# Output projection by seven products of quarters, added onto each other in PSUM

## The chip, the cores and the metric

The kernel runs on one core of one Trainium2 chip. The metric is the device time of one execution in microseconds (us); less is better. The number given for a kernel is the median over its runs.

## What is computed

One pre-norm layer of a decoder, 512 tokens of 1024 channels, all in float32, then a last norm:

```python
u = rmsnorm(x, ln1_g[i]);  proj = u @ w_in[i]          # q, k, v, pool, z, xbc, dt, gates
y_a = dilated_attention_mixer(q, k, v, rel_bias) @ w_a[i]
y_b = pool_mixer(pool_in, pool_w[i], pool_scale[i]) @ w_b[i]
y_c = ssd_mixer(...) @ w_c[i]
merged = gates[:, :, 0] * y_a + gates[:, :, 1] * y_b + gates[:, :, 2] * y_c
x = x + merged @ w_o[i]                                 # the output projection
x = x + conv_ffn(rmsnorm(x, ln2_g[i]), ...)
return rmsnorm(x, final_g)
```

The change concerns `merged @ w_o`, a product of 512x1024 by 1024x1024, and what lies next to it.

## The kernel before

**Products in three parts.** A float32 operand is split in a high half (rounded to float32r by a ScalarE cast, `cast`, L187) and a low half (operand minus high half, VectorE, `low`, L220, subtraction at L216). A product is high x high + high x low + low x high: `mm3` (L229) issues these as three sweeps over the 128-row blocks k, all added up in one PSUM bank.

**Jobs.** The work is a list of `Job`s in program order (`program`, L1442). A job has a weight piece of at most 1 MB (128 partitions x 2048) and a body. Before the body of job n, `prepare` (L1660) issues the low half of the weights of job n+1, the cast of those of n+2 (in two halves, put off to the next two calls of `step`), and the load of those of n+3. There are two buffers for raw weights, three for high halves, two for low halves. If a job is marked `late`, its body calls `prepare` itself. If it has a `then`, this runs right after its low half (L223), and a `form` gives the weights in place of a load (L190).

**Order.** The instructions of PE, ScalarE, VectorE and GpSimd go out in the order of the code; the DMA queue (SP) has an order of the scheduler. `step` (L157) runs one stretch of each generator in `running`: this is how small work is spread between blocks of matmuls.

**The stage before.** `branch_jobs(2, w_c, ..., last=True)` (L1152) has four jobs of two chunks m of 128 channels. A chunk is 24 matmuls; then VectorE multiplies by the gate (L1159), adds to the merged sum `MG[m]` (L1160), and, as this is the last branch, ScalarE and VectorE split `MG[m]` into high and low (L1163, L1164).

**The output projection** (`wo_jobs`, L1182) has eight jobs. Tokens are rows of the output, in four blocks tb of 128. For each pair of blocks and each half h of the 1024 output columns there are two jobs, one for each half of the contraction; `w_o` is thus loaded and split twice. After the second one VectorE adds the bank to the residual `X1[tb, h]` (L1185). After h = 0 follows `norm_early` (L456: ScalarE sums the squares, VectorE takes the mean, GpSimd multiplies by the gain), and after h = 1 `norm_late` (L465) and `norm_turn` (L446): scaling of both halves to `u`, eight transposes on TensorE, a ScalarE copy (L453) and a VectorE subtraction (L454). Their results are the operands of the FFN's up projection, whose first two jobs (`opening`, L1364) start with tokens 0 to 255 while the norm of the last two blocks is finished.

**Seven products.** Other parts of the kernel already form a product of 2x2 quarters by seven products (Winograd's form): `sums_of` (L319) makes the sums of the left side, `diff` (L337) differences of weight quarters, and the products' results are combined from SBUF copies (`sevens`, L341; `down_group`, L1281).

Buffers: 128x512 tiles in SBUF come from one pool of 54 (`T`, L108), PSUM banks for products from one of four (`MM`, L111), and two 1 MB buffers hold the second weight halves of a seven (`ypool`).

Of the kernel before, what the change touches and what calls it, by code (L numbers as in the profile page):

```python
# [83 lines left out]
def trunk(ctx: ExitStack, tc, out, x, rel_bias, ln1_g, w_in, b_gate, w_a, pool_w, pool_scale, w_b,  # L84
# [41 lines left out]
    waiting, running = [], []  # L126
# [99 lines left out]
    def wsrc(w, k0, k1, c0, c1):  # L226
        return w[k0 * P:k1 * P, c0:c1].rearrange("(k p) c -> p k c", p=P)

    def mm3(ps, wh, wl, xh, xl, ks, first=True, last=True, flip=False):  # L229

        n, total = 0, 3 * len(ks)
        for a, b in ((wh, xh), (wh, xl), (wl, xh)):
            for k in ks:
                l, r = (b(k), a(k)) if flip else (a(k), b(k))
                pe.matmul(ps, l, r, start=first and n == 0, stop=last and n == total - 1)  # L235
                n += 1

    def chunk_a(ps, ws, j, xh, xl, ks, lo=0, hi=S, k0=0):
# [98 lines left out]
    def diff(out, a, b):  # L337
        dve.tensor_tensor(out, a, b, OP.subtract)
        return out
# [113 lines left out]
            act.copy(hh, pv)  # L453
            dve.tensor_sub(ul[:, 4 * h:4 * h + 4, tb * P:(tb + 1) * P], pv, hh.bitcast(F32))  # L454

    def norm_early(t, g):  # L456
# [3 lines left out]
        dve.tensor_scalar(v0, ss, 1.0 / D, EPS, OP.mult, OP.add)  # L460
        pool.tensor_tensor(xg, t, g[:, :S], OP.mult)
        V0.append(v0)
        return v0, xg

    def norm_late(t, g, v0, outs, last=False):  # L465

        ss, v, sq, r, rt = (small(n, [P, 1]) for n in ("ss", "v", "sq", "r", "rt"))
        squares(act, t, ss)
        act.activation(sq, ss, AF.Sqrt, bias=v0, scale=1.0 / D)
        xg = T("xg")  # L470
        dve.tensor_tensor(xg, t, g[:, S:], OP.mult)
        dve.scalar_tensor_tensor(v, ss, 1.0 / D, v0, OP.mult, OP.add)
        yield xg
        dve.reciprocal(r, sq)
        dve.scalar_tensor_tensor(rt, r, v, r, OP.mult, OP.mult)
        dve.tensor_scalar(rt, rt, -0.5, 1.5, OP.mult, OP.add)
        if not last:
            for o, src in outs(xg):
                dve.tensor_scalar(o, src, r, rt, OP.mult, OP.mult)
# [411 lines left out]
    XS, YT, Y = {}, {}, {}  # L891
# [260 lines left out]
    def branch_jobs(b, w, parts, nk, last=False, more=()):  # L1152
        def evac(m, ps):
            if b == 1:
                MG[m] = T("yo")
                act.copy(MG[m], ps)
                return
            s = SG[b, m]
            dve.tensor_tensor(s, s, ps, OP.mult)  # L1159
            (dve if last else pool).tensor_tensor(MG[m], MG[m], s, OP.add)  # L1160
            if last:
                h, l = T("mgh", F32R), T("mgl", F32R)
                act.copy(h, MG[m])  # L1163
                dve.tensor_sub(l, MG[m], h.bitcast(F32))  # L1164
                MH[m] = (h, l)

        return jobs_a(w, 0, 8, lambda k: parts[k][0], lambda k: parts[k][1], nk, evac,
                      width=256 if nk > 4 else 512, more=more)


    X1 = {}
# [10 lines left out]
    def wo_jobs(pair, h):  # L1182
        def evac(tb, ps):
            t = X1[tb, h]
            dve.tensor_tensor(t, t, ps, OP.add)  # L1185
            if h == 0:
                nxt[tb] = norm_early(t, nxt["g2"])
                return
# [5 lines left out]
            it = norm_late(t, nxt["g2"], v0, lambda xg1: ((us[0], xg0), (us[1], xg1)))  # L1194
            next(it)

            def rest():
                next(it, None)
                yield
                norm_turn(us, nxt["uh"], nxt["ul"], tb)  # L1200

            if pair == 0:
                r = rest()
                next(r)
                running.append(after(1, r))
# [8 lines left out]
        return jobs_b(lambda k0, k1: [wsrc(w_o, k0, k1, h * S, h * S + S)], S,  # L1214
                      lambda k, tb: MH[k][0][:, tb * P:(tb + 1) * P],
                      lambda k, tb: MH[k][1][:, tb * P:(tb + 1) * P], KD, evac,
                      blocks=(2 * pair, 2 * pair + 1), turn_over=pair == 1 and h == 1)


    ACTS = {}  # L1220
# [193 lines left out]
    def early(tb):  # L1414
        yield
        fin[tb] = norm_early(X1[tb, 0], fin["g"])
# [25 lines left out]
    def program():  # L1442
        yield from jobs_a(w_in, C_POOL, 8, uhk, ulk, KD, pool_evac)
        yield Call(lambda: waiting.append(rows_of_bias()))
        yield from v_jobs(0)
        yield from qk_jobs(0)
        yield from pool_out_job()
        yield Call(lambda: attend(0))
        yield Call(lambda: waiting.insert(3, ssd_prep()))
        for i, job in enumerate(branch_jobs(1, w_b, YB, 8, more=range(7))):  # L1450
            if i == 3:
                yield Call(lambda: running.extend(after(p, sums_of_u(p)) for p in range(4)))
            yield job
# [24 lines left out]
        yield Call(finish)  # L1478
        yield from branch_jobs(2, w_c, YT, 8, last=True)
        yield Call(load_x1)  # L1480
        for pair in range(2):
            for h in range(2):
                yield from wo_jobs(pair, h)
            if pair == 0:
# [235 lines left out]
```

## Time and profile before

| what | value |
|---|---|
| median of 3 runs | 1033.97 us (1033.73 to 1034.62) |
| profiled execution, its own time | 1034.33 us |
| its span, first to last instruction | 1032.0 us |
| TensorE busy | 1021.4 us (99%) |
| VectorE busy | 714.3 us (69%) |
| ScalarE busy | 498.7 us (48%) |
| last branch's matmuls | from 583.30 us |
| output projection's matmuls | from 626.82 us |
| up projection's first matmul | 672.64 us |

A row of the timeline has start, duration, engine, line, operation, tile written <- tiles read, shapes and count; in brackets stands the idle time of the engine before it and what ended it. PE is TensorE, DVE VectorE, ACT ScalarE, POOL GpSimd, SP the queue that issues the loads. In the waits, a row has who waited for whom, the sum in us, how often, and the longest.

### The profile page before, as it was taken

Reading aid. Unit: us, or ns where it says so; the run is one execution under the profiler, and the core shown is the slowest. Engines: PE = TensorE matmul, PEld = TensorE weight load, DVE = VectorE, ACT = ScalarE, POOL = GpSimd, SP = SyncE. Lnnn points to the kernel's source line nnn. Section 1 sums busy time; section 2 is a strip of 40 time slices with the busy share of each in tenths; the row PEclk is TensorE's granted clock in tenths of the full one; section 3 lists DMA queues with packets and bytes.
Section 4 is the critical chain, followed back from the end, with each engine's and each line's share of the span. In section 5 each row is a group of like instructions: output and inputs, shape, how many; then the busy total and the mean of one; then the engine's idle time right before and its main releaser. Section 6 shows DMA issues by size and latency. Waiting matters only on the chain.

```text
span 1032.0 us, 13285 instructions
## 1 busy us (share of the span) xinstructions
PE 1021.4 (99%) x5276; PEld 858.8 (83%) x5276; DVE 714.3 (69%) x948; ACT 498.7 (48%) x800; POOL 133.5 (13%) x114
## 2 busy tenths in 40 slices
PE   9999999999999999999999999999999999999997
PEld 8998877899888887788888888898888888888885
DVE  6553566788756648666688856767778759876776
ACT  6432545454674363567575324545445544445334
POOL 1770000000000001100044501101111100111002
PEclk9999999999999999999999999999999999999999
DMA  8444312134322364551253625543231233412222
GB/s 256 148 128 139 107 57 75 31 88 137 123 82 82 94 155 110 132 144 45 79 157 121 202 82 205 175 143 114 82 123 41 85 119 98 148 41 82 82 82 82
DMA packets 112300, 115.52 MB, mean 112 GB/s; under 512 B 5203, under 2 KB 97174, under 8 KB 112239
## 3 DMA queue, kind: packets, MB, share of 16 engines
q1 hardware_dynamic: 111647, 113.83, 36.1%
q8 instruction: 41, 0.67, 0.3%
q10 hardware_dynamic: 592, 0.86, 0.2%
q14 instruction: 20, 0.16, 0.0%
HBM read 110.87 MB, written 2.22 MB: 110 GB/s over the span
## 4 chain that ended last, share of the span: by engine, by line
PE 90%; DVE 5%; ACT 3%; issue 1%; DMA 1%; ACTq 0%; DVEq 0%
PE pa L235 30%; PE pu L235 22%; PE pb L235 12%; PE pd L235 7%; PE pqk L235 6%; PE pa L1571 2%; PE pq L235 2%; PE pu L1375 1%; PE ps L740 1%; PE pt L769 1%; PE ppw L235 1%; PE po L781 1%; DVE wl L216 1%; DVE xs L1130 1%; PE py L1054 1%
## 5 line engine op out<-in xcount | busy, mean ns | idle before, releaser
L216 DVE TENSOR_TENSOR wl<-raw,wh 128x2048 fp32r<-128x2048 f32 (+3 forms) x93 | 213.5, 2297 | 47.8 <-ACT wh L196 42.7
L196 ACT CAST wh<-raw 128x1024 fp32r<-128x1024 f32 (+3 forms) x184 | 183.6, 1017 | 40.9 <-DMA raw<-in_ffn_w_down_dram 13.2
L1248 DVE SCALAR_TENSOR_TENSOR hc<-pu,fcol,hc 128x510 f32<-128x510 f32 x88 | 65.8, 748 | 48.4 <-ACT hc L1245 46.8
L235 PE MATMUL pa<-uh,wh 128*128 128x512 f32 x384 | 98.4, 398 | 0.0
L235 PE MATMUL pa<-ul,wh 128*128 128x512 f32 x384 | 94.9, 389 | 0.0
L235 PE MATMUL pa<-uh,wl 128*128 128x512 f32 x384 | 94.8, 389 | 0.0
L235 PEld LDWEIGHTS pa<-ul,wh 128*128 128x128 f32 x384 | 72.1, 188 | 15.1
L235 PEld LDWEIGHTS pa<-uh,wl 128*128 128x128 f32 x384 | 72.1, 188 | 15.0
L235 PE MATMUL pu<-uh,wh 128*128 128x512 f32 (+1 forms) x352 | 83.6, 379 | 0.0
L235 PE MATMUL pu<-uh,wl 128*128 128x512 f32 (+1 forms) x352 | 83.5, 379 | 0.0
L235 PE MATMUL pu<-ul,wh 128*128 128x512 f32 (+1 forms) x352 | 83.5, 379 | 0.0
L235 PEld LDWEIGHTS pa<-uh,wh 128*128 128x128 f32 x384 | 70.4, 188 | 14.8 <-issue 1.0
L235 PEld LDWEIGHTS pu<-ul,wh 128*128 128x128 f32 x352 | 64.2, 188 | 12.5
L235 PEld LDWEIGHTS pu<-uh,wl 128*128 128x128 f32 x352 | 64.2, 188 | 12.5
L235 PEld LDWEIGHTS pu<-uh,wh 128*128 128x128 f32 x352 | 64.1, 188 | 12.4
L1245 ACT ACTIVATE hc<-pu,fcol,fcol 128x512 f32<-128x512 f32 x40 | 31.2, 780 | 79.7 <-PE pu L235 79.7
L1253 POOL TENSOR_TENSOR hc<-hc 128x512 f32<-128x512 f32 x22 | 31.7, 1442 | 288.6 <-DVE hc L1248 253.6
L1022 POOL TENSOR_TENSOR xd<-xc,dtz 128x512 f32<-128x512 f32 x6 | 6.4, 1062 | 356.1 <-issue 307.7
L762 ACT ACTIVATE sb<-sb,nmls 128x128 f32<-128x128 f32 (+1 forms) x72 | 30.1, 419 | 30.4 <-DVE nmls L759 17.7
L1146 ACT ACTIVATE sg<-pa,col 128x512 f32<-128x512 f32 x24 | 16.5, 687 | 45.0 <-PE pa L235 44.9
L1250 ACT ACTIVATE hc<-hc 128x512 f32<-128x512 f32 x22 | 13.9, 632 | 41.0 <-DVE hc L1248 41.0
L216 DVE TENSOR_TENSOR wl<-w,wh 128x2048 fp32r<-128x2048 f32 (+1 forms) x14 | 29.9, 2135 | 5.3 <-ACT wh L196 5.3
(379 smaller groups left out, 1891.0 us busy)
## 6 DMA issues: line engine op xcount, KB each, us to landing
raw<-in_w_in_dram SPq DMA_DIRECT2D x25, 1024.0 KB, 5.4
raw<-in_ffn_w_up_dram SPq DMA_DIRECT2D x22, 1024.0 KB, 5.2
raw<-in_w_o_dram SPq DMA_DIRECT2D x8, 1024.0 KB, 6.5
raw<-in_w_in_dram SPq DMA_DIRECT2D x14, 512.0 KB, 3.9
raw<-in_ffn_w_down_dram SPq DMA_DIRECT2D x6, 1024.0 KB, 5.2
raw<-in_w_in_dram SPq DMA_DIRECT2D x6, 768.0 KB
raw<-in_w_b_dram SPq DMA_DIRECT2D x4, 1024.0 KB, 5.0
al<-ad SPq DMA_DIRECT2D x16, 256.0 KB, 7.1
```

Source lines behind the costliest of these rows:

```text
L196: act.copy(job.high[:, :, o], job.raw[:, :, o])
L216: (eng or dve).tensor_tensor(l[:, :, o], job.raw[:, :, o], h[:, :, o].bitcast(F32), OP.subtract)
L235: pe.matmul(ps, l, r, start=first and n == 0, stop=last and n == total - 1)
L740: pe.matmul(pss[i][:, o:o + w * P], q[r, n * P:(n + 1) * P], k[r, kb * P:(kb + w) * P], start=True, stop=True)
L762: act.activation(sb[:, off:off + w * P], sb[:, off:off + w * P], AF.Exp, bias=nm[:, n, h:h + 1], accum_out=ls[:, n, h:h + 1])
L769: pe.transpose(pt[:, o:o + P], sb[:, o:o + P], eye)
L1146: act.activation(s, ps, AF.Sigmoid, bias=col[:, o:o + 1])
L1245: act.activation(t, ps, AF.Identity, bias=ff["c1"][:, ff["b"] + m:ff["b"] + m + 1], scale=fw(2, m))
L1248: dve.scalar_tensor_tensor(t[:, sh:], ps[:, :S - sh], fw(k, m), t[:, sh:], OP.mult, OP.add)
L1250: act.activation(t, t, AF.Silu)
L1253: pool.tensor_tensor(a, a, t, OP.mult)
L1571: pe.matmul(first[2 * n + j][:, lo:hi], a[:, k, j * P:(j + 1) * P], b[:, k, lo:hi], start=a is wh and b is uh and k == 0, stop=a is wl and ...
```

## The change

The eight jobs of the output projection become seven. The contraction is in pairs of neighbouring 128-channel blocks (even block = first half, odd block = second half), the tokens in halves of 256 and the output columns in halves of 512. Each product is one job of two blocks of 128 tokens, 12 matmuls each. The products `two`, `five` and `three` use the two banks B, `one`, `six`, `seventh` and `four` the two banks A. `five` starts its banks afresh; `three`, `six`, `seventh` and `four` add onto what their banks hold (`onto=True`), and VectorE adds the bank's present value to the residual after every product. The weights come from four loads of 1 MB, and the differences are made in place by VectorE as `then` of four jobs. The left side's sums are made by `merged` in the steps after each pair of chunks of the last branch. The residual x is loaded one job earlier, and `ff_cols` is called before `three`. For blocks 0 and 1 the norm is finished after `six`; for 2 and 3, whose column half 1 is ready first, after `four`, with the halves' parts exchanged.

```diff
-    def mm3(ps, wh, wl, xh, xl, ks, first=True, last=True, flip=False):
+    def mm3(ps, wh, wl, xh, xl, ks, first=True, last=True, flip=False, onto=False):
+        first = first and not onto
...
             if last:
-                h, l = T("mgh", F32R), T("mgl", F32R)
-                act.copy(h, MG[m])
-                dve.tensor_sub(l, MG[m], h.bitcast(F32))
-                MH[m] = (h, l)
+                running.append(merged(m))
...
+    def merged(m):
+        a, p = MG[m], m // 2
+        if m % 2 == 0:
+            t = T("mg0", F32R)
+            act.copy(t[:, LO], a[:, LO])
+            dve.tensor_sub(t[:, HI], a[:, LO], t[:, LO].bitcast(F32))
+            MH[0, p] = (t[:, LO], t[:, HI])
+            return
+        h, l = T("mgh", F32R), T("mgl", F32R)
+        act.copy(h, a)
+        it = sums_of(MG[m - 1], a, T("msh", F32R), T("msl", F32R),
+                     lambda j, h, l: MH.__setitem__((j, p), (h, l)))
+        next(it)
+        dve.tensor_sub(l, a, h.bitcast(F32))
+        MH["A12", p] = (h[:, LO], l[:, LO])
+        MH["A22", p] = (h[:, HI], l[:, HI])
+        yield
+        yield from it
...
+        def job(j, raw, form, bank, use, more=False):
+            def body(ws):
+                wh, wl = ws
+                if not A:
+                    for b in (B, A):
+                        b.extend(MM("pb") for _ in range(2))
+                ps = {"A": A, "B": B}[bank]
+                if new.late:
+                    late_split.append(new.prepare(later=True))
+                parts = [MH[{"A11": 0}.get(j, j), p] for p in range(4)]
+                for i in range(2):
+                    o = slice(i * P, (i + 1) * P)
+                    mm3(ps[i], lambda k: wh[:, k, :], lambda k: wl[:, k, :],
+                        lambda k: parts[k][0][:, o], lambda k: parts[k][1][:, o], range(4),
+                        flip=True, onto=more)
+                    use(i, ps[i])
+                    step()
...
+        def p2(i, ps):
+            add(i, 0, ps)
+            early(i, 0)
+        def p6(i, ps):
+            add(i, 1, ps)
+            finished(i, 1)
+        def p7(i, ps):
+            add(2 + i, 1, ps)
+            early(2 + i, 1)
+        def p4(i, ps):
+            add(2 + i, 0, ps)
+            finished(2 + i, 0)
+        one = job("A11", quarter(0, 0), None, "A", lambda i, ps: add(i, 0, ps))
+        two = job("A12", quarter(1, 0), None, "B", p2)
+        five = job(1, None, lambda: one.raw, "B", lambda i, ps: add(2 + i, 1, ps))
+        three = job(4, None, lambda: W[1], "B", lambda i, ps: add(i, 1, ps), more=True)
+        six = job(2, None, lambda: one.raw, "A", p6, more=True)
+        seventh = job(3, None, lambda: W[0], "A", p7, more=True)
+        four = job("A22", None, lambda: two.raw, "A", p4, more=True)
+        one.then = lambda: diff(one.raw, W[0], one.raw)
+        five.then = lambda: diff(one.raw, W[1], one.raw)
+        three.then = lambda: diff(W[0], W[1], W[0])
+        six.then = lambda: diff(two.raw, two.raw, one.raw)
+        four.late = True
+        return load, [one, two, five, three, six, seventh, four]
...
-        yield from branch_jobs(2, w_c, YT, 8, last=True)
-        yield Call(load_x1)
-        for pair in range(2):
-            for h in range(2):
-                yield from wo_jobs(pair, h)
-            if pair == 0:
+        load, wo = wo_group()
+        yield Call(load)
+        for i, job in enumerate(branch_jobs(2, w_c, YT, 8, last=True)):
+            if i == 3:
+                yield Call(load_x1)
+            yield job
+        for i, job in enumerate(wo):
+            if i == 3:
                 yield Call(ff_cols)
+            yield job
```

In `finished`, the late norm of blocks 0 and 1 is now queued whole (`running.append(after(1, rest()))`), where before its scaling was issued at once.

More of the change, by code (lines that the diff above doesn't have):

```diff
@@ L234, in mm3 @@
                 l, r = (b(k), a(k)) if flip else (a(k), b(k))
-                pe.matmul(ps, l, r, start=first and n == 0, stop=last and n == total - 1)
+                pe.matmul(ps, l, r, start=first and n == 0, stop=last and n == total - 1,
+                          skip_group_check=onto)
                 n += 1
@@ L454, in norm_turn, with norm_early @@
             dve.tensor_sub(ul[:, 4 * h:4 * h + 4, tb * P:(tb + 1) * P], pv, hh.bitcast(F32))
-    def norm_early(t, g):
+    def norm_early(t, g, half=slice(0, S)):
         ss, v0, xg = small("ss", [P, 1]), cpool.tile([P, 1], F32, name=f"v0_{len(V0)}"), T("xg")
@@ L460, in norm_early, with norm_late @@
         dve.tensor_scalar(v0, ss, 1.0 / D, EPS, OP.mult, OP.add)
-        pool.tensor_tensor(xg, t, g[:, :S], OP.mult)
+        pool.tensor_tensor(xg, t, g[:, half], OP.mult)
         V0.append(v0)
         return v0, xg
-    def norm_late(t, g, v0, outs, last=False):
+    def norm_late(t, g, v0, outs, last=False, half=slice(S, D)):
         ss, v, sq, r, rt = (small(n, [P, 1]) for n in ("ss", "v", "sq", "r", "rt"))
@@ L470, in norm_late @@
         xg = T("xg")
-        dve.tensor_tensor(xg, t, g[:, S:], OP.mult)
+        dve.tensor_tensor(xg, t, g[:, half], OP.mult)
         dve.scalar_tensor_tensor(v, ss, 1.0 / D, v0, OP.mult, OP.add)
@@ L1180, in load_x1, with wo_group, load, add @@
                 sp.dma_start(t, x[tb * P:(tb + 1) * P, h * S:(h + 1) * S])
[L1182 to L1188, printed above, removed]
+    def wo_group():
+        quarter = lambda two, h: w_o[:, h * S:(h + 1) * S].rearrange(
+            "(k two p) c -> two p k c", two=2, p=P)[two]
+        W, A, B = [], [], []
+        def load():
+            for two in range(2):
+                W.append(ypool.tile([P, 4, S], F32, name="w3", tag="xs"))
+                sp.dma_start(W[two], quarter(two, 1))
+        def add(tb, h, ps):
+            dve.tensor_tensor(X1[tb, h], X1[tb, h], ps, OP.add)
+        def early(tb, h):
+            nxt[tb] = norm_early(X1[tb, h], nxt["g2"], slice(h * S, h * S + S))
+        def finished(tb, h):
             if "uh" not in nxt:
@@ L1193, in evac @@
             us = [T("u0"), T("u1")]
-            it = norm_late(t, nxt["g2"], v0, lambda xg1: ((us[0], xg0), (us[1], xg1)))
+            it = norm_late(X1[tb, h], nxt["g2"], v0, lambda xg: ((us[1 - h], xg0), (us[h], xg)),
+                           half=slice(h * S, h * S + S))
             next(it)
@@ L1200, in rest @@
                 norm_turn(us, nxt["uh"], nxt["ul"], tb)
-            if pair == 0:
-                r = rest()
-                next(r)
-                running.append(after(1, r))
+            if tb < 2:
+                running.append(after(1, rest()))
             elif tb == 2:
@@ L1212, in evac @@
                 late_split.pop(0)()
[L1214 to L1217, printed above, removed]
+        def job(j, raw, form, bank, use, more=False):
[15 more added lines that the diff above has]
+                    step()
+            new = Job([raw] if raw is not None else [], 4, S, body)
+            new.form = form
+            if raw is None:
+                new.load = lambda: None
+            return new
@@ L1478, in program @@
         yield Call(finish)
-        yield from branch_jobs(2, w_c, YT, 8, last=True)
-        yield Call(load_x1)
-        for pair in range(2):
-            for h in range(2):
-                yield from wo_jobs(pair, h)
-            if pair == 0:
+        load, wo = wo_group()
[6 more added lines that the diff above has]
+            if i == 3:
                 yield Call(ff_cols)
+            yield job
         loads, groups = zip(*(down_group(base) for base in range(0, KS, 8)))
```

## The prediction

> **What bounds the kernel now.** The page comes first, then the busy times by stretch for the last third's two stages.
>
> ```profile
> span 1032.0 us, 13285 instructions
> ...
> PE 1021.4 (99%) x5276; PEld 858.8 (83%) x5276; DVE 714.3 (69%) x948; ACT 498.7 (48%) x800; POOL 133.5 (13%) x114
> ...
> PEclk9999999999999999999999999999999999999999
> ...
> PE 90%; DVE 5%; ACT 3%; issue 1%; DMA 1%; ACTq 0%; DVEq 0%
> ```
>
> ```profile
> 583.30:626.82 43.52, 43.52 (x193) 36.05 (x192) 25.30 (x26) 11.01 (x14) 5.35 (x3) 1.00 0.35 115
> 626.82:672.64 45.82, 45.82 (x212) 37.94 (x210) 31.98 (x47) 24.11 (x38) 5.18 (x4) 1.00 0.59 202
> ```
>
> The columns of the second fence are the stretch, its length, and the busy time of PE, weight loads, DVE, ACT and POOL. TensorE is never idle in either, the third branch (583.30 on) or the output projection (626.82 on). So a matmul fewer is worth its full time, **as long as VectorE keeps up**. VectorE has 18.2 us free in the first stretch and 13.8 us in the second. The question is what the change does with those 32 us.
>
> The timeline of PE gives the price of the matmuls and where the stage ends:
>
> ```profile
> 626.82 1.07 PE L235 MATMUL pb<-wh,mgh 128*128 128x512 f32 x4
> 627.73 1.07 PE L235 MATMUL pb<-wh,mgl 128*128 128x512 f32 x4
> ...
> 654.03 1.91 PE L450 MATMUL uT<-eye,u 128*128 128x128 f32 x16
> ...
> 672.64 2.08 PE L1375 MATMUL pu<-uh,wh 128*128 128x256 f32 x16
> ...
> 676.47 1.04 PE L450 MATMUL uT<-eye,u 128*128 128x128 f32 x8
> 677.44 2.18 PE L1375 MATMUL pu<-uh,wl 128*128 128x256 f32 x16
> ```
>
> Four matmuls start every 0.907 us, so one costs 0.227 us and a block of 12 costs 2.72 us.
>
> **What goes.** Before: 8 jobs x 2 blocks x 12 = 192 matmuls. After: 7 x 2 x 12 = 168. 24 x 0.227 = **5.44 us** of TensorE time goes, with four 1 MB loads and one weight split.
>
> **What comes, by VectorE's queue.** The engines run in the order of the code, so I lay the new order end to end with durations of before.
>
> ```profile
> 610.71 0.69 DVE L1159 TENSOR_TENSOR sg<-sg,pa 128x512 f32<-128x512 f32 x1
> 611.50 0.69 DVE L1160 TENSOR_TENSOR yo<-yo,sg 128x512 f32<-128x512 f32 x1
> ...
> 616.14 0.69 DVE L1159 TENSOR_TENSOR sg<-sg,pa 128x512 f32<-128x512 f32 x1 [2.58 <-PE pa L235]
> ```
>
> ```profile
> 635.18 0.69 DVE L1185 TENSOR_TENSOR x<-x,pb 128x512 f32<-128x512 f32 x1 [0.37 <-PE pb L235]
> 636.66 0.15 DVE L460 TENSOR_SCALAR v<-ss 128x1 f32<-128x1 f32 x1 [0.79 <-ACT junk L437]
> ...
> 641.27 4.49 DVE L216 TENSOR_TENSOR wl<-raw,wh 128x2048 fp32r<-128x2048 f32 x2 [1.73 <-ACT wh L196]
> ...
> 649.15 0.17 DVE L474 RECIPROCAL r<-sq 128x1 f32<-128x1 f32 x1 [1.45 <-ACT sq L469]
> ...
> 649.87 1.00 DVE L479 TENSOR_SCALAR u<-xg,r,rt 128x512 f32<-128x512 f32 x2
> ...
> 656.69 2.47 DVE L454 TENSOR_TENSOR ul<-uT,uh 128x512 fp32r<-128x512 f32 x4
> ...
> 675.10 2.28 DVE L216 TENSOR_TENSOR wl<-raw,wh 128x2048 fp32r<-128x2048 f32 x1
> ```
>
> ```profile
> L323 DVE TENSOR_TENSOR sa<-hc x8: 410/412/415, 706.6 to 890.2; 128x256 f32<-128x256 f32 x8
> L326 DVE TENSOR_TENSOR sb<-hc,sa x8: 417/418/419, 707.7 to 891.4; 128x256 f32<-128x256 f32 x8
> L332 DVE TENSOR_TENSOR sal<-sa,sah x12: 679/681/687, 190.1 to 896.6; 128x512 fp32r<-128x512 f32 x12
> ```
>
> ```profile
> 922.78 2.29 DVE L216 TENSOR_TENSOR wl<-raw,wh 128x2048 fp32r<-128x2048 f32 x1 [3.15 <-ACT wh L196]
> 924.99 2.28 DVE L338 TENSOR_TENSOR w<-w,raw 128x2048 f32<-128x2048 f32 x1
> ```
>
> ```profile
> 635.90 0.63 ACT L437 ACTIVATE junk<-x 128x512 f32<-128x512 f32 x1 [3.89 <-DVE x L1185]
> 636.44 0.19 ACT L437 ACTIVATION_READ_ACCUMULATOR junk<-x 128x1 f32 x1
> ...
> 639.26 3.88 ACT L196 CAST wh<-raw 128x1024 fp32r<-128x1024 f32 x4
> ```
>
> Prices out of these. A low half or a difference of a whole weight quarter (128x2048): 2.2 us in a row. A 128x512 operation: 0.6 us, or 0.8 when the next needs its result. The four sums of a pair: 0.42 each, 1.6 together. An add followed by the row's squares: 0.69 + 0.82 of ScalarE + 0.15 = 1.66 us in which VectorE stands. The trace has no product that adds onto a bank already read. But of the 12 matmuls of a block 11 add onto their bank today, four of them to each 0.907 us, the same as for the four that hold the first; so I take 0.227 us for the twelfth too, and no range. What is new are the waits for the reads.
>
> Call the products in their order P1, P2, P5, P3, P6, P7, P4. P2, P5, P3 share two banks, and P1, P6, P7, P4 the other two. A product's first block can start only when VectorE has read the block before it in that bank. Those reads stand in VectorE's queue **behind** the low half of the next product's weights and, for P2, P5 and P3, behind a weight difference too.
>
> *Stretch 1, from 616.14 (evacuation of m = 5).* Up to the first read of P2, VectorE has: three evacuations (1.4 each, 4.2); second halves of the sums of pairs 1, 2, 3 (two splits of 0.61 each, 3.7); first halves of pairs 2 and 3 (1.6 + 0.6 each, 4.4); the split of the even chunk m = 6 with its wait for ScalarE (0.9); lows of P1, P2, P5 and differences after P1 and P5 (5 x 2.21 = 11.05); the two adds of P1 (1.2). That is 25.4 us without a pause: the read starts at 641.5 and ends at 642.2. TensorE runs P1 from 626.82 to 632.26. P2 wants its low weights at 634.07 and gets them at 634.74, so **0.7** is lost. It ends at 638.4, and P5 waits for the bank till 642.2: **3.8**.
>
> *Stretch 2.* Two adds with squares (3.3), a wait for ScalarE's cast of P3's weights, which stands behind those squares (0.9), low of P3 and a difference (4.4): the first add of P5 starts at 650.1 and ends at 650.8. P5 ended at 647.7, so P3 waits **3.2**.
>
> *Stretch 3.* Two adds, low of P6, the last difference: P3's adds start at 655.8, and P6 (other banks) starts unhindered at 656.3. P7's two blocks are followed each by the transposes of one of the first two row blocks; before, these stood at 654.03, two jobs after their inputs were begun, and waited for nothing. Now, from the end of P6 (662.2 with the two small column transposes), add, gain, reciprocal and scaling take 3.5 us for block 0: its transposes wait **0.8** behind P7's first block. For block 1, VectorE first does the low of P4 (2.2), an add with squares (1.7), a wait for ScalarE's half cast and copy (1.3), two ul splits (1.2), and the reciprocal chain with its first scaling (1.3): done at 673.8. P7 ended at 669.35, so TensorE waits **4.5**. P4 runs 674.7 to 680.1.
>
> *The next stage.* Its first low weights are wanted 4.7 us after its start, and VectorE has them ready 6.0 us after: **1.3**. Before, the low half from 675.10 was ready just when 677.44 needed it.
>
> **Sum.** 0.7 + 3.8 + 3.2 + 0.8 + 4.5 + 1.3 and 0.1 in three small places = 14.4 us of waits. The same laying-out of before's own order gives 0.9 us of waits, and ends the stage's opening at 698.1 where the trace has 697.6: it is good to half a microsecond. 14.4 - 0.9 - 5.4 = **+8.1 us**. The profiled execution took 1034.33 us (span 1032.0), which gives 1042.4; the median of the runs shown lies 0.36 us lower, and I predict 1042.1. With 2.32 us for each large operation instead of 2.21 the sum is +8.9, with 2.12 it is +7.6. Without any weight differences it would still be +3.1.
>
> Costed at nothing: the sums during the branch stage (hidden in its 18.2 us as far as 616), the loads of the second weight halves (queued before the branch; wanted only at 623), and the residual rows x, loaded earlier than before (wanted at 634.7; only after 635 would they cost, 2 us at 636).
>
> **Contention.** One operation slows VectorE in this trace:
>
> ```profile
> 584.11 3.40 DVE L216 TENSOR_TENSOR wl<-raw,wh 128x2048 fp32r<-128x2048 f32 x1
> ```
>
> ```profile
> 577.02 11.63 POOL L1160 TENSOR_TENSOR yo<-yo,sg 128x512 f32<-128x512 f32 x6 [1.23 <-DVE sg L1159]
> ```
>
> Beside GpSimd a low half takes 1.1 us longer. The four gain products on GpSimd (L461) fall beside VectorE's waits for squares in my order, so I take 0; the bound is 4 x 1.1 = 4.4 us.
>
> **Rivals.**
> *Not slower: VectorE keeps up.* If the adds stood ahead of the next low half and difference, each bank would be read 0.9 us after its block and no product would wait. Left would be P2's late weights, 0.7: 1034.0 - 5.4 + 0.7 = 1029.3. It decides from the point where stretch 1 holds under 21 us instead of 25.4. For it: 32 us of free VectorE time. Against: the order of the code, which the rows of before follow (641.27 runs two low halves before the adds). 0.05.
> *The clock falls in the waits.* The waits of PE, longest first:
>
> ```profile
> PE pa L1529 <- DVE ones L1520: 1.1, 1, 1.1
> ```
>
> The page has the clock at 9 in every slice, but TensorE's longest wait is this 1.1 us at the start, and three here are over 3. If the block after such a wait ran at half the clock, it would cost 2.72 more: one gives 1044.8, three give 1050. No row shows it. 0.10.
> The Trainium skill ("TensorE: Matmul & The Clock Gate", "Part 1: The HAM clock gate") states that the clock halves after a whole idle window of about 3.4 us and returns after a busy one. The full-clock rows here neither bear this out nor speak against it. By its window an estimate is 1.7 us for each wait that fills one.
> *Tiles run out.* I count, by the code, 53 of the 54 buffers of 128x512 in use before the last branch matmul. With two more alive, ScalarE or VectorE would wait until 626.83, when the branch's operands come free. The first such tile is wanted at 622, so up to 5 us more: 1042 to 1047. 0.07.
> *Milder.* My waits overlap better than laid out: 1036 to 1039. 0.05; within 0.2% 0.03.
> That the change does not do what it says is open only as to numbers, not time: the diff issues 168 matmuls in any case.
>
> **Chances and range.** Forecast (1039 to 1045): 0.70. The range 1038.5 to 1047 takes in the tile case, the single clock drop and GpSimd's bound. A measurement tells about 0.2% (2 us) from no change: faster 0.05, same 0.03, slower 0.92.
>
> **What would show it.** TensorE idle before the first matmul of P5 and of P3, put down to VectorE's add; idle before the second set of uT transposes, put down to the scaling; VectorE without a pause from 616 to 643; 168 matmuls on pb of this stage at 0.227 us. Wrong, if those waits are under 1 us or put down to a DMA, or if VectorE idles between 617 and 640. A granted clock under 1.00 after 642 would be the second rival.

## The result, and the profile after

| kernel | median (us) | range | runs |
|---|---|---|---|
| before | 1033.99 | 1033.16 to 1034.62 | 6 |
| after | 1042.88 | 1042.46 to 1045.78 | 6 |

The ratio is 1.0088 with a 95% interval of 1.0077 to 1.0099: the changed kernel is slower by 9.1 us (8.0 to 10.2). The forecast was 1042.1 us. The profiled execution took 1042.85 us.

The page of the changed kernel answers to the page of before line by line: span, busy times, clock, and the chain that ended last by engine.

```profile
span 1040.7 us, 13267 instructions
...
PE 1019.4 (98%) x5252; PEld 855.3 (82%) x5252; DVE 733.1 (70%) x981; ACT 501.0 (48%) x806; POOL 133.7 (13%) x114
...
PEclk9999999999999999999999999999999999999999
...
PE 85%; DVE 8%; ACT 4%; issue 1%; DMA 1%; ACTq 0%; DVEq 0%
```

TensorE has 24 matmuls fewer (5252 for 5276) and the span is 8.7 us longer. On the chain VectorE has risen from 5% to 8% of the span, though its busy time over the whole kernel went only from 69% to 70%. The page's shares hardly show why; the stretches do. Columns as before: stretch, its length, busy time of PE, weight loads, DVE, ACT and POOL, then granted clock, DMA share, GB/s.

```profile
583.30:626.82 43.52, 43.52 (x194) 36.04 (x193) 32.00 (x42) 13.38 (x19) 5.67 (x3) 1.00 0.40 137
626.82:680.00 53.18, 43.95 (x184) 34.50 (x183) 42.99 (x60) 23.14 (x37) 5.12 (x4) 0.94 0.25 81
```

The branch stage is as long as before within 0.3 us (the first product starts at 627.14 for 626.82) and TensorE is never idle in it, while VectorE does 32.0 us there for 25.3. The output projection has TensorE idle for 9.2 of 53.2 us and a granted clock of 0.94. The waits of PE (who waits for whom, sum in us, how often, the longest) name the reason:

```profile
PE pb L237 <- DVE x L1214: 4.8, 2, 3.7
PE uT L453 <- DVE u L482: 4.3, 2, 4.1
...
```

L1214 is the add that reads a bank, L482 the scaling of the normed rows. The timeline of PE shows where these waits stand. L1454 is the up projection.

```profile
627.14 1.98 PE L237 MATMUL pb<-wh,mg 128*128 128x512 f32 x8
...
634.75 1.20 PE L237 MATMUL pb<-wl,mgh 128*128 128x512 f32 x4 [0.19 <-DVE wl L216]
...
642.36 1.22 PE L237 MATMUL pb<-wh,msh 128*128 128x512 f32 x4 [3.70 <-DVE x L1214]
643.39 1.91 PE L237 MATMUL pb<-wh,msl 128*128 128x512 f32 x4
645.09 1.85 PE L237 MATMUL pb<-wl,msh 128*128 128x512 f32 x4
...
650.74 1.17 PE L237 MATMUL pb<-wh,sbh 128*128 128x512 f32 x4 [1.08 <-DVE x L1214]
...
656.30 1.07 PE L237 MATMUL pb<-wh,msh 128*128 128x512 f32 x4
...
673.26 1.29 PE L453 MATMUL uT<-eye,u 128*128 128x128 f32 x8 [4.07 <-DVE u L482]
674.21 2.06 PE L237 MATMUL pb<-wh,mgh 128*128 128x512 f32 x4
676.06 1.74 PE L237 MATMUL pb<-wh,mgl 128*128 128x512 f32 x4
...
681.30 2.08 PE L1454 MATMUL pu<-uh,wh 128*128 128x256 f32 x16
```

P5 begins at 642.36, P3 at 650.74, P6 at 656.30, P4 at 674.21. The up projection begins at 681.30 for 672.64: these 8.66 us are the whole difference of the spans. In the rows after 643.39 and after 674.21, four matmuls start every 1.57 to 1.85 us instead of 0.907.

VectorE's timeline through the first of these waits:

```profile
637.01 2.28 DVE L216 TENSOR_TENSOR wl<-raw,wh 128x2048 fp32r<-128x2048 f32 x1
639.33 2.29 DVE L341 TENSOR_TENSOR raw<-w,raw 128x2048 f32<-128x2048 f32 x1
641.54 0.68 DVE L1214 TENSOR_TENSOR x<-x,pb 128x512 f32<-128x512 f32 x1
...
649.91 1.28 DVE L1214 TENSOR_TENSOR x<-x,pb 128x512 f32<-128x512 f32 x2
```

The read of P2's first bank (641.54) stands behind the low half of P5's weights and behind a weight difference. Those rows are back to back. Since the evacuation of m = 5 VectorE has been busy in 24.37 of 25.08 us:

```profile
616.46:641.54 25.08, 22.01 (x96) 17.57 (x94) 24.37 (x31) 7.94 (x11) 0.00 (x0) 1.00 0.27 94
```

### The profile page after: what moved, and what is told of

Read it like the earlier page. It is cut to its first block, busy times and chain, and to the rows that moved or that the text cites. A ratio compares the mean times of both kernels' runs of the same rounds, so it can differ in the third digit from the quotient of the medians.

```text
span 1040.7 us, 13267 instructions
## 1 busy us (share of the span) xinstructions
PE 1019.4 (98%) x5252; PEld 855.3 (82%) x5252; DVE 733.1 (70%) x981; ACT 501.0 (48%) x806; POOL 133.7 (13%) x114
## 4 chain that ended last, share of the span: by engine, by line
PE 85%; DVE 8%; ACT 4%; issue 1%; DMA 1%; ACTq 0%; DVEq 0%
PE pa L237 28%; PE pu L237 22%; PE pb L237 9%; PE pd L237 7%; PE pqk L237 6%; PE pa L1653 2%; PE pq L237 2%; DVE wl L216 2%; PE pu L1454 1%; PE ps L743 1%; PE pt L772 1%; PE ppw L237 1%; PE po L784 1%; ACT wh L196 1%; DVE xs L1133 1%
## 5 line engine op out<-in xcount | busy, mean ns | idle before, releaser
L216 DVE TENSOR_TENSOR wl<-raw,wh 128x2048 fp32r<-128x2048 f32 (+3 forms) x90 | 206.7, 2297 | 42.0 <-ACT wh L196 38.1
L196 ACT CAST wh<-raw 128x1024 fp32r<-128x1024 f32 (+3 forms) x178 | 177.9, 1015 | 44.1 <-DMA raw<-in_ffn_w_down_dram 13.0
L216 DVE TENSOR_TENSOR wl<-w,wh 128x2048 fp32r<-128x2048 f32 (+1 forms) x16 | 34.5, 2155 | 6.1 <-ACT wh L196 6.1
L196 ACT CAST wh<-w 128x1024 fp32r<-128x1024 f32 (+1 forms) x32 | 30.3, 966 | 9.4 <-DVE w L341 5.6
```

Of the source, the lines that this page charges most:

```text
L196: act.copy(job.high[:, :, o], job.raw[:, :, o])
L216: (eng or dve).tensor_tensor(l[:, :, o], job.raw[:, :, o], h[:, :, o].bitcast(F32), OP.subtract)
```

## The experiments

Three theories were set against each other. **VectorE's queue** (A): what VectorE has to do, and the place of the bank reads and scalings in its order, makes TensorE wait. **The banks** (B): that P2, P5 and P3 share two banks, with a read in between, costs the time. **The clock** (C): the waits make the granted clock fall, and that is the loss. Each kernel stands against before, run beside it on the same chip; the runs are in three groups, in which before's median was 1034.91, 1035.08 and 1035.18 us. Edits are to the changed kernel unless said otherwise.

### No weight differences (e1_nodiff)

```diff
-        one.then = lambda: diff(one.raw, W[0], one.raw)
-        five.then = lambda: diff(one.raw, W[1], one.raw)
-        three.then = lambda: diff(W[0], W[1], W[0])
-        six.then = lambda: diff(two.raw, two.raw, one.raw)
```

> The four differences of weight quarters are left out (the products use the quarters as loaded); everything else is as in the changed kernel. Theory A (VectorE's queue: the reads of the banks come late because of what stands ahead of them): 9 us of queue go, the wait of TensorE before P5 falls from 3.7 us to about 1.6, and the clock stays full there; the wait before the second set of transposes stays near 4. Time about 4.0 us over before, 1038.0. Theory B (adding onto a bank that is read in between costs the time by itself, whatever stands ahead of the read): waits and time unchanged, 1042.9.

Measured: 1038.76 us, ratio 1.0036 (1.0022 to 1.0050), which is +3.7 us. PE's timeline shows the waits for the bank reads shrunk from 3.70 and 1.08, that for the scaling unchanged:

```profile
639.32 1.17 PE L237 MATMUL pb<-wh,msh 128*128 128x512 f32 x4 [1.34 <-DVE x L1214]
...
645.50 1.16 PE L237 MATMUL pb<-wh,sbh 128*128 128x512 f32 x4 [0.48 <-DVE x L1214]
...
668.01 1.14 PE L453 MATMUL uT<-eye,u 128*128 128x128 f32 x8 [4.05 <-DVE u L482]
```

Four operations of 2.2 us off VectorE, nothing else changed for TensorE, and more than half of the loss is gone. Part of that is the clock: behind the wait of 1.34 it stays at 1.00, where behind that of 3.70 it fell.

### P5 and P3 in banks of their own (e2_banks)

```diff
-        W, A, B = [], [], []
+        W, A, B, C = [], [], [], []
...
+                if bank == "C" and not C:
+                    C.extend(SM("pc") for _ in range(2))
-                ps = {"A": A, "B": B}[bank]
+                ps = {"A": A, "B": B, "C": C}[bank]
...
-        five = job(1, None, lambda: one.raw, "B", ...
-        three = job(4, None, lambda: W[1], "B", ...
+        five = job(1, None, lambda: one.raw, "C", ...
+        three = job(4, None, lambda: W[1], "C", ...
```

> P5 and P3 use two PSUM banks of their own, so that P5 needs no read of P2's banks. Nothing is left out. Theory A: P5 starts without a wait, but its add stands at the same place of VectorE's queue, so P3 waits about 7 us instead; with one long wait more than before the clock still falls, and the time is 1043 to 1045. Theory B: the bank waits before P5 and part of P3's go, some 4 us less: 1039.

Measured: 1046.38 us, ratio 1.0104 (1.0085 to 1.0124), +10.8 us (8.8 to 12.8). The profiled execution is the slowest of four (1043.6 to 1048.7). P5 no longer waits (its row starts at 639.35), but P3 waits longer than both did together:

```profile
639.35 1.07 PE L237 MATMUL pc<-wh,msh 128*128 128x512 f32 x4
...
651.59 2.05 PE L237 MATMUL pc<-wh,sbh 128*128 128x512 f32 x4 [6.64 <-DVE x L1214]
```

Sharing the banks is not the cause: without it the wait moves to the next product that needs a read. VectorE was no earlier for it. That the time is above the expected 1043 to 1045 fits the clock, which fell inside this wait and stood at 0.50 until 654.6, and fell again at two later waits.

### TensorE kept busy through the waits (e3_warm, e8_warm2)

Idle time is filled with matmuls whose result nobody uses. e3_warm has 8 of them before P5 and 8 after P7's second block; e8_warm2 has 14 before P5, 10 before P3 and 15 after P7's second block.

```diff
+        def busy(wh, n):
+            dm = SM("dm")
+            for _ in range(n):
+                pe.matmul(dm, wh[:, 0, :P], wh[:, 0, :], start=True, stop=True)
...
+                if j in (1, 4):
+                    busy(wh, 14 if j == 1 else 10)
...
+                    if j == 3 and i == 1:
+                        busy(wh, 15)
                     use(i, ps[i])
```

> Eight matmuls of 128x512 into a bank that nobody reads are added ahead of P5 and eight after P7's second block, so that TensorE's two longest waits become about 1.8 us shorter. Nothing is left out. Theory A: the clock stays at 1.00, P5 and P4 take 5.4 us each instead of 7.1, but P3 then waits for VectorE about 2.7 us instead of 1.1 and the up projection about 0.7 to 1.3 us for its low weights: time 0 to 1 us less, 1042.0. Theory C (the two falls of the clock are on the path): 3.3 us less, 1039.6.

Measured: 1043.14 us, ratio 1.0078 (1.0061 to 1.0095). As a test of the clock it failed, because the clock did not stay up in the profiled execution, the slowest of six (1047.04 us): the waits that were left over are shorter, but after two of the three the clock fell all the same. In two of the others the mean clock was 0.998 and the time 1041.5 and 1041.7 us.

```profile
644.83 1.21 PE L237 MATMUL pb<-wh,msh 128*128 128x512 f32 x4 [1.77 <-DVE x L1214]
...
653.31 1.16 PE L237 MATMUL pb<-wh,sbh 128*128 128x512 f32 x4 [2.70 <-DVE x L1214]
...
677.41 1.22 PE L453 MATMUL uT<-eye,u 128*128 128x128 f32 x8 [2.16 <-DVE u L482]
```

Two stretches, one behind the second and one behind the third of these rows (the clock is the third number from the end):

```profile
655.00:657.00 2.00, 2.00 (x6) 1.61 (x5) 2.00 (x2) 0.00 (x0) 0.00 (x0) 0.50 0.92 355
...
679.10:681.00 1.90, 1.90 (x6) 1.44 (x6) 0.54 (x2) 1.90 (x4) 0.74 (x1) 0.50 0.00 0
```

So the dummies were made more.

> Matmuls of 128x512 into a bank that nobody reads fill TensorE's three long waits nearly whole: 14 ahead of P5, 10 ahead of P3, 15 behind P7's second block. Nothing is left out. With no idle stretch over 1.3 us left there, the clock should stay at 1.00. Theory A (VectorE's queue sets the pace): the time stays within 1 us of the changed kernel's, 8.1 us over before. Theory C (the falls of the clock are on the path): 3.3 us less than the changed kernel, 5.6 over before.

Measured: 1042.23 us, ratio 1.0071 (1.0058 to 1.0083), +7.3 us. Now the clock is full through the stage (no wait is over 0.6 us):

```profile
626.82:680.00 53.18, 51.30 (x233) 40.93 (x232) 44.05 (x64) 23.32 (x39) 5.21 (x4) 1.00 0.24 80
```

```profile
650.10 1.20 PE L237 MATMUL pb<-wh,sbh 128*128 128x512 f32 x4 [0.37 <-DVE x L1214]
...
672.64 1.18 PE L453 MATMUL uT<-eye,u 128*128 128x128 f32 x8 [0.59 <-DVE u L482]
```

P3 starts at 650.10 for 650.74, the second set of transposes at 672.64 for 673.26. Since this execution's first product also starts 0.58 us sooner (626.56 for 627.14), both stand within 0.1 us of where they stood: with TensorE at full clock throughout, VectorE's results come when they came. Only the up projection gains: P4 runs at full clock, so it starts at 679.14, counted alike 1.6 us sooner, and then waits 0.36 us for its low weights. Of the 9.1 us some 7 remain, and the interval (6.0 to 8.6) holds theory A's 8.1 and not theory C's 5.6. The clock's falls are worth about 1.2 us by these rows and 1.8 by the medians; since the intervals of the two ratios (1.0077 to 1.0099, 1.0058 to 1.0083) overlap, that size is loose.

### Before, with one job left out (e9_one_less)

The old order, with as many matmuls as the seven products have:

```diff
-                      lambda k, tb: MH[k][1][:, tb * P:(tb + 1) * P], KD, evac,
+                      lambda k, tb: MH[k][1][:, tb * P:(tb + 1) * P], KD if pair or h else 4, evac,
```

> The kernel before, with one of the eight jobs of the output projection left out (the second half of the contraction for the first two token blocks and the first column half): 168 matmuls as in the change, the old order, no sums, no differences, one load and one weight split less. If a matmul less is worth its whole time while VectorE keeps up: 5.4 us under before, 1029. If something else paces that stage too: less than 3 us.

Measured: 1030.97 us, ratio 0.9959 (0.9945 to 0.9972), -4.2 us (-5.7 to -2.9). The profiled span is 1026.9 us, 5.1 less than before's; this execution is the fastest of four (1029.0 to 1031.8). In the stage, ended at 667.68, TensorE is never idle:

```profile
626.82:667.68 40.86, 40.85 (x186) 32.94 (x185) 29.37 (x46) 22.37 (x36) 5.18 (x4) 1.00 0.57 196
```

VectorE does 29.4 us in these 40.9; in the changed kernel it does 43.0 in 53.2. Counted from its first product (626.51 here, 626.82 in before) the stage is 4.65 us shorter, of the 5.44 counted; weight loads waited three times for a low half, 1.1 us together, which they do not in before. So the matmuls saved are worth most of what was counted, where VectorE keeps up.

### Neither sums nor differences (e5_bare)

The products take halves and quarters as they are. This drops all the arithmetic of the seven products and keeps their order.

```diff
-                running.append(merged(m))
+                merged(m)
...
-        it = sums_of(MG[m - 1], a, T("msh", F32R), T("msl", F32R),
-                     lambda j, h, l: MH.__setitem__((j, p), (h, l)))
-        next(it)
...
+        for j, half in ((1, LO), (2, HI), (3, LO), (4, HI)):
+            MH[j, p] = (h[:, half], l[:, half])
...
-        one.then = lambda: diff(one.raw, W[0], one.raw)
...
```

> Neither sums of the left side nor differences of weights: the products use halves and quarters as they are, so VectorE has the adds and the splits alone. Seven jobs and the banks as in the changed kernel. Theory A: no wait before P5 and P3; what stays are the waits of the transposes (0.8 and about 4.3), so some 1.5 us over before in spite of 24 matmuls less: 1035.5. Theory B: the bank waits stay: 1041 to 1043. If the matmuls saved were all that counts without the added work: 1028.6.

Measured: 1036.25 us, ratio 1.0013 (1.0004 to 1.0023), +1.3 us. Even so there is no gain. The banks are read in time (no wait for a read is listed); what is left is the second set of transposes and the clock after it:

```profile
666.56 1.97 PE L453 MATMUL uT<-eye,u 128*128 128x128 f32 x8 [4.07 <-DVE u L482]
668.18 2.06 PE L237 MATMUL pb<-wh,mgh 128*128 128x512 f32 x4
...
672.93 1.07 PE L237 MATMUL pb<-wh,mgh 128*128 128x512 f32 x4
```

The wait costs 4.07. The first set of transposes took 0.87 us; with these and 12 matmuls at full clock the stretch from 666.56 to 672.93 would take 3.6 us instead of 6.4. Together that is 6.9 us, more than the 5.4 saved. This wait has nothing to do with the sums and differences, which are gone here; e6_turns below moves the transposes' work in the queue and takes most of it away, so it comes from their place.

### The same work in another order (e4_mid, e6_turns, e7_order)

e4_mid: the add of a product's first block goes ahead of the next low half and difference.

```diff
-                if new.late:
+                if j == "A22":
                     late_split.append(new.prepare(later=True))
...
                     use(i, ps[i])
+                    if i == 0 and j != "A22":
+                        new.prepare()
                     step()
...
-        four.late = True
+        for one_ in (one, two, five, three, six, seventh, four):
+            one_.late = True
```

> In the first six products the low half of the next weights and the difference are issued after the first block's add instead of ahead of the product; the same instructions in another order, nothing left out. Theory A: the place in the queue is part of the cost: P5's and P3's first blocks wait no more, their second blocks wait 1.9 and 1.5 us, no clock fall; about 4.9 us over before, 1038.9. If only the amount of VectorE's work counted: 1042 to 1043.

Measured: 1041.53 us, ratio 1.0058 (1.0043 to 1.0073), +6.0 us.

```profile
644.07 1.21 PE L237 MATMUL pb<-wh,msh 128*128 128x512 f32 x4 [1.73 <-DVE x L1214]
...
670.67 1.97 PE L453 MATMUL uT<-eye,u 128*128 128x128 f32 x8 [3.17 <-DVE u L482]
```

P5's first block waits for no read any more; this is its second, and the wait is half of the 3.70. The miss against the expected 1038.9 lies, by these rows, mainly in the clock, which fell in the wait of 3.17 and stood at half until 676.6 (the rows are in the last section).

e6_turns: in P7 and P4 the pending norm work goes ahead of the add of the block.

```diff
+                    if j in (3, "A22"):
+                        step()
+                        use(i, ps[i])
+                        continue
                     use(i, ps[i])
                     step()
```

> In the last two products (P7, P4) the small work that is spread between blocks (transposes, their splits, the scaling) is issued ahead of the add of the same block instead of behind it. The same instructions, nothing left out. Theory A: the second set of transposes waits about 1.5 us instead of 4.1, no clock fall at P4, P4's second block waits 1.4: about 6.8 us over before, 1040.8. If the time lost before the transposes only moves on to the up projection's start: 1042.9.

Measured: 1043.01 us, ratio 1.0078 (1.0061 to 1.0095), +8.1 us. Expected were 1040.8, so this is a miss. The wait it was aimed at went from 4.07 to 1.17, and the up projection begins 3.1 us earlier (678.20). But in this execution (1043.90 us) all of that is given back one stage on, where TensorE waits for ScalarE's copy of the transposes, and the clock falls behind that wait:

```profile
670.12 1.11 PE L453 MATMUL uT<-eye,u 128*128 128x128 f32 x8 [1.17 <-DVE u L482]
...
678.20 2.08 PE L1458 MATMUL pu<-uh,wh 128*128 128x256 f32 x16
...
694.18 1.23 PE L237 MATMUL pu<-uh,wh 128*128 128x256 f32 x8 [1.92 <-ACT uh L456]
```

e7_order: both, and the row mean of the early norm is put off by one step, so that VectorE does not stand still for ScalarE's squares.

```diff
+                    if j in (3, "A22"):
+                        step()
+                        use(i, ps[i])
+                        if i == 0 and j == 3:
+                            new.prepare()
+                        continue
                     use(i, ps[i])
+                    if i == 0:
+                        new.prepare()
                     step()
...
-        dve.tensor_scalar(v0, ss, 1.0 / D, EPS, OP.mult, OP.add)
+        def mean(n):
+            for _ in range(n):
+                yield
+            dve.tensor_scalar(v0, ss, 1.0 / D, EPS, OP.mult, OP.add)
```

> The orders of the two kernels before this one together (next weights' low half and difference behind the first add; transposes ahead of the add), and the small mean after the squares put off by one step, so that VectorE doesn't stand for ScalarE. Nothing left out. Theory A: 2.6 us over before, 1036.6, with VectorE busy nearly without a pause from 616 to 680: the order recovers two thirds of the loss, and the amount of VectorE's work the rest. If order were all: below 1034.

Measured: 1038.28 us, ratio 1.0037 (1.0023 to 1.0051), +3.8 us. Not one operation of the change is left out here, and 5.3 of the 9.1 us are gone by order alone. What is left may be the amount of VectorE's work. Busy times from 616 to 682 us (DVE is the third), of e7_order and then of the changed kernel as it was:

```profile
616.00:682.00 66.00, 60.88 (x283) 48.86 (x282) 60.27 (x86) 30.47 (x50) 9.00 (x4) 0.97 0.32 112
```

```profile
616.00:682.00 66.00, 56.77 (x242) 45.22 (x241) 54.81 (x78) 26.44 (x43) 5.12 (x4) 0.95 0.30 102
```

In the better order VectorE is busy for 60.3 of 66 us, in the changed kernel for 54.8, so it has little left to give. That the rest of the loss is amount is not shown by this: TensorE still waits up to 1.86 us at a time here, and the clock falls once.

### Work moved to GpSimd (e10_pool, e11_pool2)

e10_pool is e7_order with the four sums of a pair on GpSimd; e11_pool2 moves the difference after P3 there as well, in four pieces of 128x512.

```diff
...
-        dve.tensor_tensor(sa[:, LO], f0[:, HI], f1[:, HI], OP.add)
+        eng.tensor_tensor(sa[:, LO], f0[:, HI], f1[:, HI], OP.add)
...
-        three.then = lambda: diff(W[0], W[1], W[0])
+        def pieces():
+            for k in range(4):
+                pool.tensor_tensor(W[0][:, k, :], W[1][:, k, :], W[0][:, k, :], OP.subtract)
+        three.then = pieces
```

> The last order kernel (next weights' low half and difference behind the first add, transposes ahead of the add, the small mean put off) with the sixteen sums of 128x256 of the left side on GpSimd instead of VectorE; nothing left out. Theory A: 6 us of VectorE's queue go, the product P2 waits no more for its weights and P5 less: 1.5 to 2 us under the last order kernel, if GpSimd's work doesn't hold VectorE up. If each of GpSimd's operations holds VectorE up by about a microsecond, as beside the branch's sums in the profile of before: no gain.

> As the kernel with the sums on GpSimd, and the difference after P3 on GpSimd too, in four pieces of 128x512; nothing left out. Theory A: P3's second block waits no more: a further 1.4 us less, about the time of before. If GpSimd holds VectorE up: as the kernel with the sums on GpSimd, or slower.

Measured: 1037.57 us, ratio 1.0027 (1.0015 to 1.0039), and 1038.36 us, ratio 1.0037 (1.0023 to 1.0050). The sums are worth about 1 us against e7_order, within the intervals, for 1.5 to 2 expected (P2 still waits 0.6 us for its low weights, 0.8 in e7_order); the difference is worth nothing, for 1.4 expected. In e11_pool2 GpSimd takes 7.07 us for what VectorE does in 2.29, and VectorE's low half beside it takes 3.03 for 2.28:

```profile
645.44 7.07 POOL L1312 TENSOR_TENSOR w<-w,w 128x512 f32<-128x512 f32 x4
...
645.85 3.03 DVE L216 TENSOR_TENSOR wl<-w,wh 128x2048 fp32r<-128x2048 f32 x1 [1.07 <-ACT wh L196]
```

No version of the seven products tried beats before; the best that leaves nothing out, e10_pool, is 2.8 us (1.6 to 4.0) slower.

## Why the prediction was right

**What goes: 5.44 us.** Right within the interval. e9_one_less has 5.1 us less span in its profiled execution, the fastest of four, and -4.2 us (-5.7 to -2.9) over all.

**What comes: 14.4 us of waits.** From after's rows, the path has 0.5 for P2's low weights (its last four matmuls start at 637.60 where 637.11 was due), 3.7 before P5, 1.1 before P3, 0.2 and 4.1 before the two sets of transposes: 9.5 us. Two falls of the clock add 3.4. With 0.3 at the start and 0.9 in places under 0.3 that makes 14.1, and 14.1 - 5.4 = 8.7, the difference of the spans. So the sum held, but not by its own terms alone:

| step of the prediction | forecast | measured |
|---|---|---|
| P2, low weights | 0.7 | 0.5 |
| P5, wait for the bank read | 3.8 | 3.70 |
| P3, wait for the bank read | 3.2 | 1.08 |
| P5 itself, at a lowered clock | 0 | 1.7 |
| P6, no wait | 0 | 0 |
| first set of transposes | 0.8 | 0.2 |
| second set of transposes | 4.5 | 4.07 |
| P4, at a lowered clock | 0 | 1.65 |
| up projection's low weights | 1.3 | 0 |

**The order of VectorE's queue.** Right to within a few tenths: the read behind a low half and a difference was forecast to start at 641.5 and started at 641.54; P3's at 650.1 and started at 649.91; P6 at 656.3 and started at 656.30. It was shown from both sides: less work in the same order (e1_nodiff, +3.7) and the same work in a better order (e7_order, +3.8) each take away more than half, and other banks (e2_banks, +10.8) take away nothing. "Without any weight differences it would still be +3.1" stands against +3.7 measured (2.3 to 5.2).

**The clock in the waits.** Given 0.10 and left out of the sum; by the prediction's own sign, a granted clock under 1.00 after 642, it happened, and twice. These are the stretches of the changed kernel after the waits of 3.70 and 4.07:

```profile
643.40:645.10 1.70, 1.70 (x6) 1.32 (x5) 0.51 (x2) 1.70 (x4) 1.45 (x2) 0.50 0.00 0
645.10:646.80 1.70, 1.70 (x6) 1.34 (x5) 1.30 (x1) 1.70 (x3) 0.08 (x1) 0.52 0.00 0
...
674.20:676.00 1.80, 1.80 (x6) 1.48 (x5) 0.21 (x2) 1.71 (x4) 1.28 (x1) 0.50 0.00 0
676.00:677.60 1.60, 1.60 (x5) 1.24 (x4) 1.14 (x2) 0.92 (x2) 0.00 (x0) 0.54 0.00 0
```

Half the clock for 3.4 us costs 1.7 us, not the 2.72 of a whole block. The forecast held in spite of it, in part because of what follows. P5 ran 1.7 us longer, and P3 had to wait for VectorE anyway: its wait shrank from 3.2 to 1.08, and e8_warm2, at full clock throughout, has P3 at the same place. This fall cost nothing. P4 ran 1.65 longer, and that much later the up projection found its low weights ready; but at full clock it waits only 0.36 for them, so about 1.2 us of this fall reached the end. The forecast lacks them, and waits that came out smaller than laid out make up for them (before the transposes 0.2 and 4.07 for 0.8 and 4.5; for the low weights 0.36 at full clock for 1.3). That the sum came within 1 us is therefore luck in part; that most of the loss is VectorE's queue is not: some 7 of the 9 us remain in e8_warm2.

The Trainium skill ("TensorE: Matmul & The Clock Gate", "Part 1: The HAM clock gate") puts a fall behind a whole idle window of about 3.4 us, on a grid that runs on by itself, and the return behind a busy one. The length agrees with the rows (3.4 us at 0.50); the condition does not, since the clock fell after 2.70 and 2.16 us in e3_warm.

**GpSimd's gain products, costed at nothing.** Right in the changed kernel: they fell beside VectorE's waits, and the reads stand within 0.2 us of the forecast. **Tiles running out.** Did not happen: VectorE idles 0.7 of 25.1 us from 616.46 on, and the branch stage ends 0.3 us late.

## What to carry to other kernels

Where one engine is never idle, work saved on it counts in full only as long as the others keep up, and that is read from the queue of each in the stretch that changes, not from busy shares of the whole kernel: here VectorE's 70% hid a stretch at 97%. Before making a product depend on a read of its bank, lay out what stands in the reader's queue ahead of that read, and put long work that nobody waits for behind it; order alone was worth 5.3 us here. And look past the product itself: a step pulled closer to its inputs can by itself undo the saving (the transposes in e5_bare: 4.1 us of waiting and 2.8 at half clock behind it, for 5.4 saved).

## What the runs showed of the hardware

**The clock falls in steps of 3.4 us, and waits of 1.9 us can be enough.** The stretches here show a clock of 1.00, of 0.50, or a mean of the two. In one with a mean, the share at half clock is twice what is missing to 1.00, and that gives the moment of the change. Two stretches of e4_mid, around the wait that ended at 670.67:

```profile
668.00:670.67 2.67, 0.00 (x0) 0.00 (x1) 2.49 (x8) 0.00 (x0) 0.00 (x0) 0.84 0.44 120
...
676.00:677.00 1.00, 1.00 (x5) 0.79 (x4) 0.00 (x0) 0.00 (x0) 0.00 (x0) 0.69 0.00 0
```

The clock fell at 670.67 - 2 x 0.16 x 2.67 = 669.8 and came back at 676.6, 6.8 us later. In the changed kernel it fell at 643.3 and 674.1 and came back after 3.4 us both times; these two falls are 30.7 us apart, 9 times 3.4. So the clock seems to be decided at points 3.4 us apart. For each wait, the step of 3.4 us in which it lay (laid out from the fall, or where the clock stayed up from the next fall in the same kernel):

| kernel, wait | idle time within one step | clock after it |
|---|---|---|
| after, 4.07 | 2.6 | falls |
| after, 3.70 | 2.4 | falls |
| e3_warm, 2.70 | 2.2 | falls |
| e3_warm, 2.16 | 2.2 | falls |
| e6_turns, 1.92 | 1.9 | falls |
| e7_order, 1.86 | 1.9 | falls |
| e4_mid, 1.73 | 1.6 | stays |
| e3_warm, 1.77 | 1.2 | stays |

In these eight the clock falls behind a step that is idle for 1.9 of 3.4 us or more and stays up behind 1.6 or less, so about half a step seems to decide. In e4_mid the fall comes inside the wait, and the way back takes a second step. A step at half clock full of matmuls costs 1.7 us. That the decision goes by such a share is a reading of these rows; no run moved a wait within its step to try it.

**GpSimd and VectorE hold each other up on float32 sums.** In e10_pool a sum of 128x256 on GpSimd takes 0.74 us in one place and 2.79 in another, where VectorE runs a low half that takes 2.82 for 2.28:

```profile
600.96 0.74 POOL L330 TENSOR_TENSOR sb<-yo,sa 128x256 f32<-128x256 f32 x1
...
610.60 2.79 POOL L330 TENSOR_TENSOR sb<-yo,sa 128x256 f32<-128x256 f32 x1
...
609.97 2.82 DVE L216 TENSOR_TENSOR wl<-raw,wh 128x2048 fp32r<-128x2048 f32 x1
...
640.40 3.26 DVE L342 TENSOR_TENSOR raw<-w,raw 128x2048 f32<-128x2048 f32 x1
```

The last row is a weight difference on VectorE; it takes 3.26 us for 2.29 while GpSimd has a gain product (638.24 to 641.51). So GpSimd's idle time (87% of the span of the changed kernel) is not free room for VectorE's work.

**Adding onto a bank that VectorE has read cost nothing by itself here.** P3 adds onto P5's banks and takes 5.56 us from 650.74 to 656.30, for 24 matmuls of 0.227 (5.44). Only the wait for the reader counts.
